# The map from the conditions in steps of two row blocks by 1536 columns, with the next step's loads issued behind each step

## The chip, the cores and the metric

The kernel runs on one core of a Trainium2 chip. The metric is the device time of one execution in microseconds (us). Engine names are those of the profile: PE is TensorE (matmuls; PEld is its weight load), DVE is VectorE, ACT is ScalarE, POOL is GpSimd, SP is the engine whose queue issues the DMAs.

## The reference, cut to what matters

A two-layer trunk over 512 latent and 256 context tokens (768 in all, width 1024). Each layer is FFN, mixer, FFN, and every sub-layer is modulated by shift, scale and gate vectors that are a linear map of two condition vectors (`c` and `c_ctx`):

```
def ada_mod(cond, w, b):                      # w: 1024 x 9216 for each layer
    m = jax.nn.silu(cond) @ w + b
    return m.reshape(m.shape[:-1] + (N_MOD, D_MODEL))

def ffn_half(h, m, j, g, w1, w3, w2):
    u = modulate(rmsnorm(h, g), m[:, :, 3 * j], m[:, :, 3 * j + 1])
    return h + 0.5 * m[:, :, 3 * j + 2] * swiglu(u, w1, w3, w2)
```

The change concerns `ada_mod`: two rows times a matrix of 1024 x 9216 float32, twice. The matrices are 36 MB each in memory and all of them has to be read; the arithmetic is small.

## The kernel before

All activations lie feature-major, with 384 tokens as one chunk. A matmul of the FFNs is done as three matmuls on split operands (`mm3`, lines L197, L198 and L199: high x high, high x low, low x high), 128x128 weights against 384 columns. Weights come from HBM as tiles of 128 x 1024 (`load`, L151, tile name raw) and are split in two by ACT (L191) and DVE (L192) into blocks (blk); POOL forms sums of weight quarters first (`seven`, L574, tile name S). An FFN (`ffn`, L628) goes over 11 groups of two hidden tiles: for each group `up` with w1 (seven products of 12 matmuls), `down` of the group before (96 matmuls), and `up` with w3. The gated values of a group lie in tiles g, from a pool of six.

The map from the conditions is spread over the two FFNs of layer 0 as filling work: FFN(0, 0) carries the rest of layer 0's map (columns 2048 to 9216), FFN(0, 1) all of layer 1's. `ada_round(l, col, ncol)` (L242) is a generator. It goes over the eight row blocks k of 128 rows; for each it loads the row block's columns in tiles of 128 x 1024 (L253, tile name ada, two of them for 2048 columns) and does four matmuls (L257) with the 32-wide stationary operand `sc[:, k, :]`. The four take a quarter of the columns each and write PSUM partitions 0, 32, 64 and 96 of one bank, so that they use four different column groups of the array. A float32 matmul of this kind has two records in the profile: a step of four shows as x8. After the eighth row block `ada_out` copies the bank to SBUF (DVE, L270, tile adasb), transposes it by quarters of 128 columns on PE (L272) and adds the bias (L275).

What sets the order: `ffn` calls `step()` behind every product of `up` and behind every second row of `down`; each `every`-th call advances the generator by one `yield`, that is, by one row block. `every` is 4; in FFN(0, 0) it is 2 in the first group and 1 in the `up` of the second. FFN(0, 0) runs one round of 1024 columns (the gate, which its own first `down` needs) and three of 2048, FFN(0, 1) four of 2048 and one of 1024: 32 and 40 row blocks. The loads of a row block stand in the program at the row block's own matmuls. The two ada tiles come from the pool `more` (two tiles of 128 x 1024), so a load has to wait until the matmuls that read its tile before are through. SP issues all loads in one queue, the weights' and the map's, and a DMA that waits for its tile holds those behind it. The order within each engine is then laid down at build time by a list scheduler, which may move an instruction ahead of or behind others by its own model of when its operands are there.

Of the kernel before, what the change touches and what calls it, by code (L numbers as in the profile page):

```python
# [9 lines left out]
F32 = mybir.dt.float32  # L10
F32R = mybir.dt.float32r
# [5 lines left out]
P = 128  # L17
D = 1024
KD = 8
# [6 lines left out]
NMOD = 9  # L26
# [63 lines left out]
class Builder:  # L90
# [58 lines left out]
    def load(self, src, pool=None):  # L149
        raw = (pool or self.rawp).tile([P, 1024], F32, tag="raw", name=self.name("raw"))  # L150
        self.nc.sync.dma_start(out=raw[:, :src.shape[-1]], in_=src)  # L151
        return raw
# [86 lines left out]
        nc.sync.dma_start(out=self.xs[1], in_=t["xT"][:, :, SEQ:TOK])  # L239


    def ada_round(self, l, col, ncol):  # L242

        nc, t = self.nc, self.t
        w = ncol // 4
        nq = w // P
        ps = self.aux_ps()
        for k in range(KD):

            raws = []  # L250
            for c0 in range(0, ncol, 1024):
                raws.append(self.ada_tile())
                nc.sync.dma_start(  # L253
                    out=raws[-1], in_=t["ada_w"][l, k * P:(k + 1) * P, col + c0:col + c0 + 1024])
            for g in range(4):
                c = g * w
                nc.tensor.matmul(  # L257
                    ps[32 * g:32 * g + 32, :w], self.sc[:, k, :], raws[c // 1024][:, c % 1024:c % 1024 + w],
                    start=(k == 0), stop=(k == KD - 1),
                )  # L260
            yield
        b0 = col // P
        view = lambda x: x[..., b0:b0 + 4 * nq].rearrange("p (s g q) -> p s g q", s=2, g=2)
        self.ada_out(l, ps, w, self.aux_ps(), view)

    def ada_out(self, l, ps, w, pt, view):

# [360 lines left out]
    def ffn(self, l, s, T, after, ready=None, chs=CH2, fill=(), start=None):  # L628
        nc, t = self.nc, self.t
        fill = list(fill)  # L630
        gate = lambda cond, d: self.gh[l][s][:, cond, d:d + 1]
        w = chs[0][1]
# [9 lines left out]
        def step(every=4):  # L642
            turns[0] += 1
            if turns[0] % every == 0:
                next(todo, None)

        with ExitStack() as st:
            self.psum(mm=6)
            pool = lambda name, bufs: st.enter_context(
                self.tc.tile_pool(name=self.name(name), bufs=bufs, reuse_waits="tile"))  # L650
# [2 lines left out]
            self.blocks_in("AAAABBBBB", pool("blkB", 5))  # L653

            whole = chs is CHX2
            gp = pool("g", 4 if whole else 6)
            self.sums = pool("sums", 2)

            more = pool("more", 2)
            nraw = 5  # L660
            if fill:
                self.adap, nraw = more, 3
# [66 lines left out]
            for n in range(NG):  # L729
                last = n == NG - 1  # L730
                g = [[None, None] for _ in range(2)]
# [12 lines left out]
                def room():  # L744
                    if whole:
                        for i in range(2):
                            both = gp.tile([P, 2, 2 * w], F32R, tag="g", name=self.name("g"))
                            g[i] = [both[:, :, :w], both[:, :, w:], both]
                        return
                    for c in range(2):  # L750
                        for i in range(2):
                            g[i][c] = gp.tile([P, 2, w], F32R, tag="g", name=self.name("g"))


                often = lambda: step((2, 1)[n] if n < 2 and start is not None else 4)
                def results(c, fs, ps):
                    for (i, z), p in zip(fs, ps):
                        (first if z == "w1" else second)(i, c, p[:, :w])
                        often()
# [7 lines left out]
                if n == 0:  # L767

                    room()
                    fs = [(i, z) for i in range(2) for z in ("w1", "w3")]  # L770
                    if start is None:
# [5 lines left out]
                    else:  # L777
# [5 lines left out]
                        ps = [self.mm_ps() for _ in fs]  # L783
# [14 lines left out]
                else:  # L798
                    self.up(blocks, T, w, first, often)
                    items = [take(2) for _ in pending], of(pending)  # L800
                    self.down(*items, chs[:1] if last else CHX if whole else chs, gate, step=step)
                    room()
                    self.up(blocks, T, w, second, often)
                if last:
# [667 lines left out]
    def run(self):  # L1472
        t = self.t
        self.setup()
        self.load_x()
        T, begin = self.halves(0, 0, two=True)

        def start():

            begin(*CH2[0])  # L1480
            slot = lambda: self.slot([P, 1024], F32, "ada")
            self.ada_tile = lambda: self.adap.tile([P, 1024], F32, tag="raw", name=self.name("ada"))
            for _ in self.ada_half(0, [slot] * 8):
                pass
            self.now()
            yield
            raw = lambda: self.rawp.tile([P, 1024], F32, tag="raw", name=self.name("ada"))
            half = self.ada_half(1, [slot] * 4 + [raw] * 3 + [self.ada_tile])
            next(half)
            yield  # L1490
            next(half, None)
            yield
            self.load_rest()
            begin(*CH2[1])
            yield

        def rounds(l, first):
            for col in range(first, NMOD * D, 2048):
                yield lambda col=col: self.ada_round(l, col, min(2048, NMOD * D - col))

        def gate():
            yield from self.ada_round(0, 2048, 1024)
            self.ada_gh(0, 0)

        def derive(l):
            def f():
                self.ada_gh(l, 1)
                for j in range(1 - l, 3):
                    self.ada_sp(l, j)
                if l:  # L1510
                    self.ada_gh(1, 0)
            return f

        ffn = lambda l, s: self.ready([t["w1"][l, s, 0], t["w3"][l, s, 0]])
        nxt, after = self.norm(0, 1)
        ready = self.ready([t["ein"][12 + i] for i in range(2)])
        self.ffn(0, 0, T, after, ready, fill=[gate, *rounds(0, 3072), derive(0)], start=start)
        u, (nxt, after) = nxt, self.halves(0, 2)
        self.even_mixer(u[0], after, ffn(0, 1))
        u, (nxt, after) = nxt, self.halves(1, 0)  # L1520
        self.ffn(0, 1, u, after, ffn(1, 0), fill=[*rounds(1, 0), derive(1)])
        u, (nxt, after) = nxt, self.norm(1, 1)
        self.ffn(1, 0, u, after, self.ready([t["oin"][1 + i, 0] for i in range(2)]))
        u, (nxt, after) = nxt, self.halves(1, 2)
        self.odd_mixer(u[0], after, ffn(1, 1))
        self.ffn(1, 1, nxt, self.final(), chs=CHX2)
        self.now()
# [96 lines left out]
```

## Time and profile before

| | |
|---|---|
| time, three runs | 2882.99 us median (2879.05 to 2884.05) |
| the profiled execution | 2885.63 us, span 2883.8 us |
| PE busy | 2798.5 us (97%), 17014 instructions |
| DVE, ACT, POOL busy | 72%, 42%, 17% |
| granted PE clock | 0.99 |
| DMA | 266.38 MB, 92 GB/s over the span |

The map's matmuls stand between 49.2 and 1379.4 us. Three stretches are used below: 100 to 212 us (the first two rounds of 2048 columns, in FFN(0, 0)), 212 to 290 us (the third), and 990 to 1390 us (layer 1's map, in FFN(0, 1)).

### The profile page before, as it was taken

To read this page: it belongs to the slowest core of one execution; us is meant where nothing else is said; L and a number is where in the kernel's file an instruction comes from. 1 tells how busy PE (TensorE), PEld (TensorE's weight loads), DVE (VectorE), ACT (ScalarE), POOL (GpSimd) and SP (SyncE) were. 2 spreads that over 40 slices of the span, in tenths; PEclk is the share of its full clock that TensorE was granted. 3 is DMA by queue.
4 is the path that set the end of the run, shared out by engine and by line. 5 is a ranking of instruction groups with operands and counts; after the bars stand their busy time and mean duration, and the time that the engine had idled before them with its cause. 6 is when DMAs were issued, how large, how long until landed. Compare 5 with 4: busy or idle time off the path is not lost.

```text
span 2883.8 us, 43969 instructions
## 1 busy us (share of the span) xinstructions
PE 2798.5 (97%) x17014; PEld 2603.0 (90%) x17014; DVE 2079.2 (72%) x3994; ACT 1220.1 (42%) x2406; POOL 481.5 (17%) x358
## 2 busy tenths in 40 slices
PE   6999999999999999999999999999999999889998
PEld 5678999999977888889999999999989989789998
DVE  5646777776677776666778777777855565799998
ACT  4323333352166632332336333323564565554443
POOL 0211222200000022121211222222000000133331
PEclk9999999999999999999999999999999999999999
DMA  7564121221110244443221221221121111122332
GB/s 258 162 197 167 59 81 59 70 72 59 54 34 16 74 175 154 175 168 125 96 81 37 81 74 59 81 66 59 61 75 59 59 67 52 66 81 95 110 103 74
DMA packets 81458, 266.38 MB, mean 92 GB/s; under 512 B 8416, under 2 KB 13920, under 8 KB 81248
## 3 DMA queue, kind: packets, MB, share of 16 engines
q1 hardware_dynamic: 81248, 263.56, 26.6%
q8 instruction: 134, 2.20, 0.3%
q14 instruction: 76, 0.62, 0.1%
HBM read 261.43 MB, written 2.10 MB: 91 GB/s over the span
## 4 chain that ended last, share of the span: by engine, by line
PE 87%; DVE 7%; ACT 3%; issue 1%; POOL 1%; DMA 1%; POOLq 0%; SPq 0%; DVEq 0%; ACTq 0%
PE mm L197 27%; PE mm L199 26%; PE mm L198 26%; PE aux L257 3%; DVE blk L192 1%; DVE xx L447 1%; PE o L1040 1%; POOL S L574 1%; DMA ada<-in_ada_w 1%; DVE acc L371 1%; PE aux L1028 1%; PE aux L350 0%; PE ds L1273 0%; PE o L1295 0%; PE aux L1268 0%
## 5 line engine op out<-in xcount | busy, mean ns | idle before, releaser
L192 DVE TENSOR_TENSOR blk<-raw,blk 128x512 fp32r<-128x512 f32 (+1 forms) x617 | 469.2, 769 | 182.9 <-ACT blk L191 175.6
L191 ACT ACTIVATE blk<-raw 128x512 fp32r<-128x512 f32 (+1 forms) x617 | 379.7, 625 | 485.2 <-PE mm L199 417.4
L191 ACT ACTIVATE blk<-S 128x512 fp32r<-128x512 f32 x320 | 201.6, 630 | 560.4 <-PE mm L199 528.6
L197 PE MATMUL mm<-g,blk 128*128 128x384 f32 (+2 forms) x1264 | 429.0, 341 | 3.9 <-ACT blk L191 3.9
L199 PE MATMUL mm<-g,blk 128*128 128x384 f32 (+2 forms) x1264 | 428.2, 339 | 0.0
L198 PE MATMUL mm<-g,blk 128*128 128x384 f32 (+2 forms) x1264 | 427.9, 339 | 0.0
L447 DVE SCALAR_TENSOR_TENSOR xx<-mm,gh,xx 128x384 f32<-128x384 f32 (+3 forms) x600 | 307.3, 519 | 150.4 <-PE mm L199 141.7
L192 DVE TENSOR_TENSOR blk<-S,blk 128x512 fp32r<-128x512 f32 x320 | 252.4, 790 | 90.0 <-ACT blk L191 84.1
L603 DVE TENSOR_TENSOR t<-t,mm 128x384 f32<-128x384 f32 (+1 forms) x400 | 206.8, 517 | 113.2 <-PE mm L199 112.2
L197 PEld LDWEIGHTS mm<-g,blk 128*128 128x128 f32 x1264 | 237.2, 188 | 27.3 <-issue 7.1
L199 PEld LDWEIGHTS mm<-g,blk 128*128 128x128 f32 x1264 | 237.5, 188 | 9.4 <-issue 3.4
L198 PEld LDWEIGHTS mm<-g,blk 128*128 128x128 f32 x1264 | 237.8, 188 | 8.2 <-issue 2.5
L197 PE MATMUL mm<-uH,blk 128*128 128x384 f32 (+1 forms) x648 | 225.9, 353 | 1.8 <-ACT uH L387 1.7
L198 PE MATMUL mm<-uL,blk 128*128 128x384 f32 (+1 forms) x648 | 222.6, 345 | 0.0
L199 PE MATMUL mm<-uH,blk 128*128 128x384 f32 (+1 forms) x648 | 221.9, 345 | 0.0
L574 POOL TENSOR_TENSOR S<-raw 128x512 f32<-128x512 f32 x80 | 114.1, 1426 | 583.5 <-DMA raw<-in_w 399.9
L574 POOL TENSOR_TENSOR S<-raw,raw 128x512 f32<-128x512 f32 x80 | 106.2, 1328 | 458.2 <-DVE blk L192 457.2
L574 POOL TENSOR_TENSOR S<-S,raw 128x512 f32<-128x512 f32 x80 | 109.9, 1374 | 319.5 <-issue 314.4
L191 ACT ACTIVATE g<-t 128x384 fp32r<-128x384 f32 (+1 forms) x176 | 87.1, 497 | 129.8 <-DVE t L741 128.6
L197 PEld LDWEIGHTS mm<-uH,blk 128*128 128x128 f32 x648 | 121.1, 188 | 10.3 <-ACT uH L387 3.1
L199 PE MATMUL mm<-T11H,blk 128*128 128x384 f32 (+1 forms) x384 | 126.1, 329 | 3.9 <-DVE blk L192 3.9
L197 PE MATMUL mm<-T21H,blk 128*128 128x384 f32 (+1 forms) x384 | 125.8, 330 | 3.8 <-ACT t L608 1.9
(282 smaller groups left out, 6937.9 us busy)
## 6 DMA issues: line engine op xcount, KB each, us to landing
raw<-in_w SPq DMA_DIRECT2D x256, 512.0 KB, 3.3
ada<-in_ada_w SPq DMA_DIRECT2D x144, 512.0 KB, 4.4
raw<-in_oin SPq DMA_DIRECT2D x32, 512.0 KB, 3.2
raw<-in_w SPq DMA_DIRECT2D x32, 256.0 KB, 2.8
raw<-in_ein SPq DMA_DIRECT2D x16, 512.0 KB, 3.3
raw<-in_eout SPq DMA_DIRECT2D x8, 512.0 KB, 3.2
raw<-in_oi SPq DMA_DIRECT2D x8, 512.0 KB, 3.2
raw<-in_oout SPq DMA_DIRECT2D x8, 512.0 KB, 3.2
```

Source lines behind the costliest of these rows:

```text
L191: self.nc.scalar.activation(out=hi, in_=src, func=AF.Copy)
L192: (eng or self.nc.vector).tensor_tensor(out=lo, in0=src, in1=hi.bitcast(F32), op=ALU.subtract)
L197: nc.tensor.matmul(out, aH, bH, start=start, stop=False, skip_group_check=more)
L198: nc.tensor.matmul(out, aH, bL, start=False, stop=False, skip_group_check=more)
L199: nc.tensor.matmul(out, aL, bH, start=False, stop=stop, skip_group_check=more)
L257: nc.tensor.matmul(ps[32 * g:32 * g + 32, :w], self.sc[:, k, :], raws[c // 1024][:, c % 1024:c % 1024 + w], start=(k == 0), stop=(k == KD ...
L371: nc.vector.tensor_tensor(out=acc[:, :w], in0=acc[:, :w], in1=dst[:, :w], op=ALU.add)
L447: nc.vector.scalar_tensor_tensor(out=xv, in0=ps[:, off:off + m], scalar=gate(cond, d), in1=xv, op0=ALU.mult, op1=ALU.add,)
L574: nc.gpsimd.tensor_tensor(out=out, in0=a, in1=b, op=op)
L603: add = lambda out, a, b: nc.vector.tensor_tensor(out=out, in0=a, in1=b, op=ALU.add)
L1028: nc.tensor.transpose(pt[:, k * P:(k + 1) * P], pr[:, (k0 + k) * P:(k0 + k + 1) * P], self.ident)
L1040: nc.tensor.matmul(o[64 * e:64 * e + 64, :256], V[kt // 3][:, kt % 3, c:c + 64], s.PT[e][:, k, :], start=k == 0, stop=k == nk - 1)
```

## The change

`ada_round` becomes `ada_rounds(l, jobs)`. A job is a range of columns and a function to call when its values are there; FFN(0, 0) has one job of 1024 and four of 1536 columns, FFN(0, 1) six of 1536. A step is two row blocks (eight matmuls) of one tile each, so an FFN has 20 and 24 steps. The loads of the next step, also the next job's, stand behind the matmuls of a step. `ada_out` follows at once behind a job's last step instead of at the next `yield`. The ada tiles are 128 x 1536 (two, in `more`); the pool g has four tiles in these two FFNs instead of six, and the last group's gated values of the second chunk lie in the two tiles of `more`. `step()` advances the map every second call in the first group and every sixth call of `up` afterwards; the calls in `down` stay at every fourth. Outside these two FFNs the order of every engine is the same as before.

```diff
-    def ada_round(self, l, col, ncol):
+    def ada_rounds(self, l, jobs):
...
-        for k in range(KD):
+        def load(col, ncol, k):
             raws = []
-            for c0 in range(0, ncol, 1024):
+            for kk in (k, k + 1):
                 raws.append(self.ada_tile())
                 nc.sync.dma_start(
-                    out=raws[-1], in_=t["ada_w"][l, k * P:(k + 1) * P, col + c0:col + c0 + 1024])
-            for g in range(4):
-                c = g * w
-                nc.tensor.matmul(
-                    ps[32 * g:32 * g + 32, :w], self.sc[:, k, :], raws[c // 1024][:, c % 1024:c % 1024 + w],
-                    start=(k == 0), stop=(k == KD - 1),
-                )
+                    out=raws[-1][:, :ncol], in_=t["ada_w"][l, kk * P:(kk + 1) * P, col:col + ncol])
+            return raws
+
+        steps = [(*job, k) for job in jobs for k in range(0, KD, 2)]
+        raws = load(*steps[0][:2], 0)
+        for i, (col, ncol, done, k0) in enumerate(steps):
+            w = ncol // 4
+            if k0 == 0:
+                ps = self.aux_ps()
+            for k, raw in zip((k0, k0 + 1), raws):
+
+                for g in range(4):
+                    nc.tensor.matmul(
+                        ps[32 * g:32 * g + 32, :w], self.sc[:, k, :], raw[:, g * w:(g + 1) * w],
+                        start=(k == 0), stop=(k == KD - 1),
+                    )
+            if i + 1 < len(steps):
+                raws = load(*steps[i + 1][:2], steps[i + 1][3])
+            if k0 == KD - 2:
+                b0, nq = col // P, w // P
+                view = lambda x: x[..., b0:b0 + 4 * nq].rearrange("p (s g q) -> p s g q", s=2, g=2)
+                self.ada_out(l, ps, w, self.aux_ps(), view)
+                if done:
+                    done()
             yield
...
-            gp = pool("g", 4 if whole else 6)
+            gp = pool("g", 4 if whole or fill else 6)
...
+            lent = lambda: (more if fill else gp).tile(
+                [P, 2, w], F32R, tag="raw" if fill else "g", name=self.name("g"))
...
-                            g[i][c] = gp.tile([P, 2, w], F32R, tag="g", name=self.name("g"))
+                            g[i][c] = lent() if last and c else gp.tile(
+                                [P, 2, w], F32R, tag="g", name=self.name("g"))
...
-                often = lambda: step((2, 1)[n] if n < 2 and start is not None else 4)
+                often = lambda: step(2 if n == 0 else 6)
...
-            self.ada_tile = lambda: self.adap.tile([P, 1024], F32, tag="raw", name=self.name("ada"))
+            self.ada_tile = lambda: self.adap.tile([P, 1536], F32, tag="raw", name=self.name("ada"))
...
-        self.ffn(0, 0, T, after, ready, fill=[gate, *rounds(0, 3072), derive(0)], start=start)
+        self.ffn(0, 0, T, after, ready, fill=[rounds(0, [(2048, 1024, lambda: self.ada_gh(0, 0))])], start=start)
...
-        self.ffn(0, 1, u, after, ffn(1, 0), fill=[*rounds(1, 0), derive(1)])
+        self.ffn(0, 1, u, after, ffn(1, 0), fill=[rounds(1, [])])
```

Three places in the order of the instructions. Names carry the buffers' numbers; aux is the map's PSUM bank, mm a bank of the FFN.

PE, FFN(0, 0), in the first `down` (the matmuls on g), where the first 2048-column round runs before and the first 1536-column job now. Before:

```order
L198 MATMUL mm_180_1035<-g_7_130,blk_160_932 128x384
L257 MATMUL aux_155_917<-ada_165_973,sc_85 32x512 x2
L199 MATMUL mm_180_1035<-g_7_130,blk_160_932 128x384
L197 MATMUL mm_180_1035<-g_8_131,blk_168_985 128x384
L198 MATMUL mm_180_1035<-g_8_131,blk_168_985 128x384
L199 MATMUL mm_180_1035<-g_8_131,blk_168_985 128x384
L257 MATMUL aux_155_917<-ada_166_975,sc_85 32x512 x2
L197 MATMUL mm_181_1043<-g_7_130,blk_164_958 128x384
```

In the changed kernel, at the same place:

```order
L198 MATMUL mm_184_1080<-g_10_133,blk_166_977 128x384
L199 MATMUL mm_184_1080<-g_10_133,blk_166_977 128x384
L264 MATMUL aux_155_904<-ada_175_1019,sc_85 32x384 x4
L264 MATMUL aux_155_904<-ada_176_1021,sc_85 32x384 x4
L197 MATMUL mm_187_1101<-g_9_132,blk_162_940 128x384
L198 MATMUL mm_187_1101<-g_9_132,blk_162_940 128x384
```

The four matmuls of one row block, which stood in two pairs with four of the FFN's between them, now stand together, and the next row block's four stand right behind them.

PE, FFN(0, 0), at the end of the first group, where the gate's 1024 columns end. Before, the last three row blocks:

```order
L257 MATMUL aux_89_483<-ada_141_816,sc_85 32x256 x3
L197 MATMUL mm_129_780<-T1H_100_541,blk_138_796 128x384
L198 MATMUL mm_129_780<-T1L_101_542,blk_138_796 128x384
L257 MATMUL aux_89_483<-ada_144_840,sc_85 32x256 x4
L197 MATMUL mm_130_781<-T2H_114_623,blk_140_801 128x384
L198 MATMUL mm_130_781<-T2L_115_624,blk_140_801 128x384
L257 MATMUL aux_89_483<-ada_146_861,sc_85 32x256 x4
L257 MATMUL aux_89_483<-ada_150_886,sc_85 32x256 x4
```

In the changed kernel, from the gate's last step on:

```order
L264 MATMUL aux_91_487<-ada_123_716,sc_85 32x256 x4
L264 MATMUL aux_91_487<-ada_124_718,sc_85 32x256 x4
L197 MATMUL mm_136_815<-T11H_41_235,blk_145_829 128x384
L198 MATMUL mm_136_815<-T11L_42_236,blk_145_829 128x384
L197 MATMUL mm_137_816<-T1H_104_557,blk_146_832 128x384
L198 MATMUL mm_137_816<-T1L_105_558,blk_146_832 128x384
L197 MATMUL mm_138_817<-T2H_118_639,blk_148_837 128x384
L198 MATMUL mm_138_817<-T2L_119_640,blk_148_837 128x384
L284 MATMUL aux_130_787<-ident_81,adasb_131_788 128x128 x2
L264 MATMUL aux_155_904<-ada_128_783,sc_85 32x384 x4
```

The gate's transposes (L284, the former L272) and the first row block of the next job now stand six of the FFN's matmuls behind the gate's last step; before, the transposes stood 55 rows behind it.

SP, the same time: the loads of the gate's last row blocks and of the round or job behind it. Before:

```order
L253 DMA ada_146_861<-in_ada_w 128x1024
L253 DMA ada_150_886<-in_ada_w 128x1024
L253 DMA ada_156_918<-in_ada_w 128x1024
L253 DMA ada_157_920<-in_ada_w 128x1024
L151 DMA raw_158_928<-in_w2 128x1024
L151 DMA raw_159_930<-in_w3 128x1024
L151 DMA raw_167_983<-in_w3 128x1024
L151 DMA raw_170_991<-in_w1 128x1024
L253 DMA ada_161_947<-in_ada_w 128x1024
L253 DMA ada_162_949<-in_ada_w 128x1024
```

In the changed kernel:

```order
L251 DMA ada_124_718<-in_ada_w 128x1024
L251 DMA ada_128_783<-in_ada_w 128x1536
L251 DMA ada_129_785<-in_ada_w 128x1536
L251 DMA ada_156_913<-in_ada_w 128x1536
L151 DMA raw_160_936<-in_w2 128x1024
L151 DMA raw_161_938<-in_w3 128x1024
L151 DMA raw_165_975<-in_w3 128x1024
L251 DMA ada_157_915<-in_ada_w 128x1536
L151 DMA raw_168_983<-in_w1 128x1024
```

A weight tile of the next `down` (raw_160, before raw_158) now stand behind the first load of a job's second step, which waits for the matmuls on ada_128.

## Rows read from the trace of the kernel before

**Rows 1.** The page's first part (busy us, share of the span, instructions) and the lines of its chain of work that ended last.

```profile
PE 2798.5 (97%) x17014; PEld 2603.0 (90%) x17014; DVE 2079.2 (72%) x3994; ACT 1220.1 (42%) x2406; POOL 481.5 (17%) x358
...
PE mm L197 27%; PE mm L199 26%; PE mm L198 26%; PE aux L257 3%; DVE blk L192 1%; DVE xx L447 1%; PE o L1040 1%; POOL S L574 1%; DMA ada<-in_ada_w 1%; DVE acc L371 1%; PE aux L1028 1%; PE aux L350 0%; PE ds L1273 0%; PE o L1295 0%; PE aux L1268 0%
```

**Rows 2.** Busy time by stretch, all engines (columns: stretch, its us, then busy us and instructions of PE, PEld, DVE, ACT, POOL, then granted PE clock, DMA share, GB/s).

```profile
100.00:212.00 112.00, 108.44 (x547) 75.81 (x547) 54.55 (x106) 24.09 (x43) 21.53 (x16) 0.98 0.59 194
...
990.00:1390.00 400.00, 398.36 (x2341) 356.27 (x2342) 270.33 (x519) 134.60 (x254) 79.55 (x60) 1.00 0.44 154
```

**Rows 3.** The same stretches for the map's matmuls alone (L257; busy us of PE and PEld, then clock, DMA share, GB/s).

```profile
100.00:212.00 112.00, 31.41 (x128) 4.26 (x128) 0.98 0.59 194
212.00:290.00 78.00, 8.52 (x64) 1.26 (x64) 1.00 0.47 162
990.00:1390.00 400.00, 40.24 (x320) 6.42 (x320) 1.00 0.44 154
```

**Rows 4.** PE in order of time (start, us, instruction; xN counts records): a step of 512 columns whose four matmuls stand together, between the FFN's.

```profile
222.65 0.33 PE L197 MATMUL mm<-T4H,blk 128*128 128x384 f32 x1
...
223.00 0.34 PE L199 MATMUL mm<-T4H,blk 128*128 128x384 f32 x1
223.27 1.06 PE L257 MATMUL aux<-ada,sc 128*32 128x512 f32 x8
...
224.54 0.34 PE L198 MATMUL mm<-T11L,blk 128*128 128x384 f32 x1
```

**Rows 5.** The same view, a step in two halves.

```profile
115.18 0.34 PE L198 MATMUL mm<-g,blk 128*128 128x384 f32 x1
115.45 1.05 PE L257 MATMUL aux<-ada,sc 128*32 128x512 f32 x4
116.43 0.45 PE L199 MATMUL mm<-g,blk 128*128 128x384 f32 x1
116.71 0.34 PE L197 MATMUL mm<-g,blk 128*128 128x384 f32 x1
...
117.34 1.05 PE L257 MATMUL aux<-ada,sc 128*32 128x512 f32 x4
```

**Rows 6.** The same view: a step of 256 columns; and, ahead of it in the program, 31 matmuls of 256 columns in a row (L295, the part of the map that is done before FFN(0, 0)).

```profile
1324.12 0.34 PE L199 MATMUL mm<-T2H,blk 128*128 128x384 f32 x1
1324.38 0.64 PE L257 MATMUL aux<-ada,sc 128*32 128x256 f32 x8
...
1325.24 0.34 PE L198 MATMUL mm<-T21L,blk 128*128 128x384 f32 x1
...
36.58 3.65 PE L295 MATMUL mm<-ada,sc 128*32 128x256 f32 x62
```

**Rows 7.** The same view: three of PE's four waits for a load of the map, and what follows (in brackets the idle time ahead and what ended it).

```profile
85.35 0.64 PE L257 MATMUL aux<-ada,sc 128*32 128x256 f32 x8 [1.69 <-DMA ada<-in_ada_w]
87.28 1.08 PE L257 MATMUL aux<-ada,sc 128*32 128x256 f32 x8 [1.29 <-DMA ada<-in_ada_w]
88.29 0.69 PE L199 MATMUL mm<-T11H,blk 128*128 128x384 f32 x1
...
90.69 0.34 PE L197 MATMUL mm<-T11H,blk 128*128 128x384 f32 x1
...
107.35 1.59 PE L257 MATMUL aux<-ada,sc 128*32 128x512 f32 x4 [2.58 <-DMA ada<-in_ada_w]
108.87 0.69 PE L199 MATMUL mm<-T4H,blk 128*128 128x384 f32 x1
...
110.45 1.37 PE L257 MATMUL aux<-ada,sc 128*32 128x512 f32 x4
```

**Rows 8.** PE's waits from 45 to 300 us (us in total, times, longest).

```profile
PE aux L257 <- DMA ada<-in_ada_w: 6.5, 4, 2.6
```

**Rows 9.** The copy of a finished bank on DVE, its neighbours there, and the transposes behind it on PE; then a set of transposes that stands alone.

```profile
1236.34 1.14 DVE L192 TENSOR_TENSOR blk<-raw,blk 128x512 fp32r<-128x512 f32 x1
...
1237.86 0.68 DVE L270 COPY adasb<-aux 128x512 f32<-128x512 f32 x1
...
1238.60 0.66 PE L272 MATMUL aux<-ident,adasb 128*128 128x128 f32 x4 [0.18 <-DVE adasb L270]
...
289.82 0.34 PE L199 MATMUL mm<-T22H,blk 128*128 128x384 f32 x1
290.00 0.60 PE L272 MATMUL aux<-ident,adasb 128*128 128x128 f32 x4
...
290.61 0.34 PE L198 MATMUL mm<-T4L,blk 128*128 128x384 f32 x1
```

**Rows 10.** SP in order of time (its DMA issues), the loads' median time to landing from 990 to 1390 us, and a POOL instruction that waits for the weights issued at 1086.48.

```profile
1085.58 0.80 SPq L253 DMA_DIRECT2D ada<-in_ada_w  x2
1086.48 0.37 SPq L151 DMA_DIRECT2D raw<-in_w  x1
...
ada<-in_ada_w SPq DMA_DIRECT2D x70, 512.0 KB, 4.2
raw<-in_w SPq DMA_DIRECT2D x48, 512.0 KB, 3.5
...
1091.93 1.29 POOL L574 TENSOR_TENSOR S<-raw 128x512 f32<-128x512 f32 x1 [6.83 <-DMA raw<-in_w]
```

**Rows 11.** Who waited for whom from 1000 to 1390 us, the largest wait (us in total, times, longest).

```profile
ACT blk L191 <- PE mm L199: 195.7, 71, 13.4
```

More of the change, by code (lines that the diff above doesn't have):

```diff
@@ L239, in load_rest @@
         nc.sync.dma_start(out=self.xs[1], in_=t["xT"][:, :, SEQ:TOK])
-    def ada_round(self, l, col, ncol):
+    def ada_rounds(self, l, jobs):
         nc, t = self.nc, self.t
-        w = ncol // 4
-        nq = w // P
-        ps = self.aux_ps()
-        for k in range(KD):
+        def load(col, ncol, k):
             raws = []
-            for c0 in range(0, ncol, 1024):
+            for kk in (k, k + 1):
                 raws.append(self.ada_tile())
                 nc.sync.dma_start(
-                    out=raws[-1], in_=t["ada_w"][l, k * P:(k + 1) * P, col + c0:col + c0 + 1024])
-            for g in range(4):
-                c = g * w
-                nc.tensor.matmul(
-                    ps[32 * g:32 * g + 32, :w], self.sc[:, k, :], raws[c // 1024][:, c % 1024:c % 1024 + w],
-                    start=(k == 0), stop=(k == KD - 1),
-                )
+                    out=raws[-1][:, :ncol], in_=t["ada_w"][l, kk * P:(kk + 1) * P, col:col + ncol])
[20 more added lines that the diff above has]
+                    done()
             yield
-        b0 = col // P
-        view = lambda x: x[..., b0:b0 + 4 * nq].rearrange("p (s g q) -> p s g q", s=2, g=2)
-        self.ada_out(l, ps, w, self.aux_ps(), view)
     def ada_out(self, l, ps, w, pt, view):
@@ L1487, in start @@
             raw = lambda: self.rawp.tile([P, 1024], F32, tag="raw", name=self.name("ada"))
-            half = self.ada_half(1, [slot] * 4 + [raw] * 3 + [self.ada_tile])
+            half = self.ada_half(1, [slot] * 4 + [raw] * 3 + [lambda: self.ada_tile()[:, :1024]])
             next(half)
@@ L1495, in start, with rounds, derive @@
             yield
[L1497 to L1506, printed above, removed]
+        def rounds(l, jobs):
+            def derive():
                 self.ada_gh(l, 1)
@@ L1511, in f @@
                     self.ada_gh(1, 0)
-            return f
+            first = jobs[-1][0] + jobs[-1][1] if jobs else 0
+            jobs = jobs + [(col, 1536, None) for col in range(first, NMOD * D, 1536)]
+            jobs[-1] = *jobs[-1][:2], derive
+            return lambda: self.ada_rounds(l, jobs)
         ffn = lambda l, s: self.ready([t["w1"][l, s, 0], t["w3"][l, s, 0]])
```

## The prediction

> **What bounds the kernel now.** I read the engines' totals first: PE is busy 97% of the span, and the chain that ended last is made of its matmuls, 3% of it the map's [rows 1]. So time is won only where PE does less or waits less. The stretches come next. In 990 to 1390 us, where layer 1's map runs, PE is busy 398.4 of 400 us while DVE has 270 and ACT 135; from 100 to 212 us it is busy 108.4 of 112 [rows 2]. PE is the limit in both, and what the change takes from PE there is time, as long as the weights still come. The reader should then look at how the map's matmuls lie between the FFN's: what counts is how often PE is interrupted, more than how many columns it is given.
>
> **What an interruption costs.** Take the start of the FFN matmul ahead of a run of the map's and the start of the second one behind it, less two ordinary spacings. An ordinary spacing is 0.175 us (222.65 to 223.00 us for two). A run of four matmuls of 512 columns costs 224.54 - 223.00 - 0.35 = 1.19 us [rows 4]. A run of only two of the four costs 116.71 - 115.18 - 0.35 = 1.18 us, and its other half comes at 117.34 and costs as much again [rows 5]: the four column groups work side by side, so half a step costs a whole one. Four matmuls of 256 columns cost 1325.24 - 1324.12 - 0.35 = 0.77 us. From 256 to 512 columns the price rises by 0.42 us, so the fixed part of a run is 0.35 us. Where 31 matmuls of 256 columns stand in a row (62 records) they take 3.65 us, that is 0.47 us for four [rows 6]: nearly the 0.42 of the columns, with the fixed part paid once. Four of 384 columns alone therefore cost 0.35 + 0.63 = 0.98 us, and eight in a row 0.35 + 1.26 = 1.61 us (estimates from these rows).
>
> A rule that speaks against the change: the Trainium skill, TensorEngine Tiling (Array Packing), section Performance Considerations, says that each matmul carries some 60 cycles of its own. The change makes 352 matmuls of the map out of 288 for the same columns; by the page's figure 64 more would be an estimated 1.6 us at 2.4 GHz, and the sum below would be smaller by that. The 31 in a row show no such part per matmul, so I don't take it.
>
> **PE's work, part by part.** The columns are the same before and after; the runs are not.
> - FFN(0, 0), the 2048-column rounds: 24 row blocks in 37 runs (14 in the first round, first at 100.01 us; 15 in the second; 8 in the third). The busy time says so too: 31.4 us for the 16 row blocks of the first two rounds against 8.5 us for the 8 of the third [rows 3]. 37 x 1.19 = 44.0 us. In the changed order 15 of the 16 steps of 1536 columns stand in one run and the other in three: 15 x 1.61 + 3 x 0.98 = 27.1 us. Gain 16.9 us.
> - The gate's 1024 columns: nine runs of 0.77, now five and two double ones (0.77 + 0.42): 6.9 to 6.2, gain 0.7 us.
> - FFN(0, 1): 33 runs of 512 and 8 of 256 columns, 39.3 + 6.2 = 45.5 us (busy 40.2 [rows 3], the rest being the spacing lost around them). Now 22 of 24 steps in one run and two in two each: 22 x 1.61 + 4 x 0.98 = 39.3 us. Gain 6.2 us.
>
> Together 23.8 us. The transposes are the same 32 tiles in 11 sets instead of 9; a set of four alone takes 290.61 - 289.82 - 0.35 = 0.44 us, 0.11 each, with no fixed part [rows 9], so more sets cost nothing.
>
> **The waits that go.** PE waited four times, 6.5 us in all, for a load of the map [rows 8], all in FFN(0, 0). Behind a wait it runs at half speed for a while: from 88.29 to 90.69 us seven matmuls take 2.40 us instead of 1.3, the run at 87.28 takes 1.01 instead of 0.57, the run at 107.35 1.52 instead of 0.98, and the four behind it 1.58 instead of 0.9 [rows 7]. That is the lower of the two clock levels, 1.2 instead of 2.4 GHz, and another 2.8 us. With the loads a step ahead, and 10 to 15 us between steps (50 or 75 FFN matmuls and a run), against a median landing of 4.2 us [rows 10], these 9.3 us go.
>
> **The waits that come.** Two.
> - The first 1536-column step stands six FFN matmuls and two transposes behind the gate's last step, whose tiles its loads need. They can be issued only when the gate's matmuls are through, and PE is there about 2 us later (six spacings, the transposes and the wait for their copy); a load takes 3.5 to 4.2 us from issue to landing [rows 10] and is half as long again here. The wait is 0 to 3.5 us; I take 1.5, nearer to the short landing, and 1.3 for half speed behind it. Queued behind PE is the whole FFN; on SP the weights behind `ada_156` wait too, but those are for the next `down`, seven products later.
> - The transposes now stand five FFN matmuls (0.9 us) behind a job's last step and need DVE's copy. Copying 512 columns takes 0.68 us, and PE waited 0.18 us for one that DVE reached late [rows 9]. For 384 columns DVE needs about 0.55 us and just makes it when it is free; if it has just begun its longest neighbour (1.14 us [rows 9]) PE loses about 1.0 us. Eleven sets: 0 to 11 us; I take 0.2 each, 2.2 us, as in the row that shows such a wait.
>
> The smaller pool g costs nothing: a group's tiles are written behind the `down` that frees them, four products of the next `up` later. The `more` tiles that the last group borrows are free by then, since 24 steps end in about the sixth group. The loads have the same bytes.
>
> **The sum.** 2885.6 - 23.8 - 6.5 - 2.8 + 1.5 + 1.3 + 2.2 = 2857.5 us against the profiled execution, 28.1 us less. The median of the runs lies 2.6 us below that execution: **2855 us**.
>
> **Rivals.**
> - *The new waits eat half.* Every copy comes late (11 us) and the map's loads are waited for as before (9.3 us): 2883 - 23.8 - 9.3 + 11 + 9.3 = 2870 us. For it: DVE is busy 68% where the map runs. Against it: in `down`, where most jobs end, DVE only drains PSUM rows that PE finished before the run.
> - *Two row blocks don't share a run.* Each pays its own 0.35 us: 37 x 0.35 = 13 us less gain, 2868 us. Against it speak the 31 in a row [rows 6].
> - *The change doesn't bring what it should:* PE's freed time comes back as waits for weights that ACT, DVE or POOL deliver no faster than now; 2880 us. Against it: ACT waited 195.7 us for PE to free a block between 1000 and 1390 us [rows 11], so it is ahead.
> - *Slower: weights behind the map's loads.* SP issues in one queue. A weight tile issued behind two loads of 512 KB at 1086.48 let POOL begin at 1091.93, 5.45 us later, against a median landing of 3.5 [rows 10]: 2 us for 1 MB, so 3 us for the 1.5 MB now (estimate). And up to two steps' loads now stand between two weight tiles, so that the second is held for 10 to 15 us more. It costs only where ACT's lead is used up: from there, some 20 weight tiles (two of six in each of the ten groups with map) 2.5 us late would be 50 us: 2883 - 28 + 50 = 2905 us. By the Trainium skill, DMA: Bandwidth & Descriptors, section Queues, rings and completion order, descriptors of one queue are taken in ring order, so that what stands behind waits; the 5.45 us agree. ACT's waits for PE, up to 13.4 us [rows 11], speak against it.
>
> **How the numbers follow.** Forecast 0.67, new waits 0.12, no shared runs 0.08, nothing gained 0.07, slower 0.06. A measurement of this kernel can tell about 0.2%, 5.8 us. Faster by more than that are the first three, 0.87; within it 0.07; slower 0.06. The forecast's own ends are 2850 (no new wait at all) and about 2865; three us below for the spread of the runs, and up through the two rivals at 2868 and 2870 with some room: 2847 to 2876.
>
> **What would show it.** In the changed profile the map's runs should read x16, with some 1.4 us from their start to the next FFN matmul and 1.6 us by the rule of three starts above; in the stretches of rows 3 the map's matmuls should fall from 80 to about 60 busy us. PE's waits for the map's loads should be one or two near the end of the first group. A wait of PE for adasb at the 11 transposes shows the copies' price. ACT waiting for the weights' DMA instead of PE, and PE for blk, would show the slower case. The prediction is wrong if runs of eight cost two runs, or if PE's idle time grows by more than 10 us between 80 and 1400 us.

## The result, and the profile after

The changed kernel takes 2854.01 us (median of 4 runs, 2852.49 to 2856.89) against 2882.3 us of the kernel before on the same chip (2879.05 to 2884.05): 28.3 us less, a ratio of 0.9903 [0.9891, 0.9915]. The profiled execution took 2852.72 us and its span is 2850.9 us, 32.9 us less than the span before. The forecast was 2855 us.

The first lines to read are the engines' totals and the chain that ended last, to be laid beside [rows 1].

```profile
PE 2771.3 (97%) x17142; PEld 2605.0 (91%) x17142; DVE 2082.8 (73%) x4000; ACT 1218.7 (43%) x2406; POOL 479.9 (17%) x358
...
PE mm L197 27%; PE mm L198 26%; PE mm L199 26%; PE aux L264 2%; DVE blk L192 1%; DVE xx L459 1%; PE o L1056 1%; POOL S L586 1%; PE aux L1044 1%; PE aux L362 1%; PE o L1311 1%; PE ds L1289 0%; PE aux L1284 0%; ACT blk L191 0%; PE aux L339 0%
```

PE has 128 more records and 27.2 us less busy time; its idle time in the span went from 85.3 to 79.6 us. So 27 of the 33 us are busy time of PE, not waits: 17.2 up to the end of FFN(0, 0), 6.9 in the stretch with FFN(0, 1), and 3.1 in stretches where the two kernels have the same order. The other engines do what they did. In the chain the map's matmuls went from 3 to 2%, and the map's loads, 1% before, are gone from it.

The next line groups the map's matmuls (us busy and mean ns, then the idle time ahead of them); before, the same view had 86.8 us for x576 at L257.

```profile
L264 PE MATMUL aux<-ada,sc 128*32 128x384 f32 (+1 forms) x704 | 68.3, 487 | 1.7 <-DMA ada<-in_ada_w 1.7
```

The same weights pass PE in 18.5 us less. Of the rest of the 27.2 us, the 3.1 of the unchanged stretches owe nothing to the change; some 5.6 lie in the FFN's matmuls around the runs (the spacing that each interruption stretches) and in those that ran at the lower clock.

Now PE in order of time, four places: a step of the map between the FFN's matmuls, a step that was cut in two, the transposes of a finished bank, and the end of the gate with the first step of the next job.

```profile
143.77 0.34 PE L199 MATMUL mm<-T4H,blk 128*128 128x384 f32 x1
144.03 1.50 PE L264 MATMUL aux<-ada,sc 128*32 128x384 f32 x16
145.46 0.44 PE L197 MATMUL mm<-T11H,blk 128*128 128x384 f32 x1
145.74 0.34 PE L198 MATMUL mm<-T11L,blk 128*128 128x384 f32 x1
...
1196.48 0.34 PE L199 MATMUL mm<-T11H,blk 128*128 128x384 f32 x1
1196.75 0.85 PE L264 MATMUL aux<-ada,sc 128*32 128x384 f32 x8
...
1197.82 0.34 PE L198 MATMUL mm<-T1L,blk 128*128 128x384 f32 x1
...
285.58 0.34 PE L198 MATMUL mm<-g,blk 128*128 128x384 f32 x1
285.75 0.49 PE L284 MATMUL aux<-ident,adasb 128*128 128x128 f32 x3
...
286.26 0.33 PE L197 MATMUL mm<-g,blk 128*128 128x384 f32 x1
...
84.53 0.34 PE L198 MATMUL mm<-T2L,blk 128*128 128x384 f32 x1
85.71 0.44 PE L284 MATMUL aux<-ident,adasb 128*128 128x128 f32 x2 [0.85 <-DVE adasb L282]
87.51 1.25 PE L264 MATMUL aux<-ada,sc 128*32 128x384 f32 x8 [1.36 <-DMA ada<-in_ada_w]
89.35 0.69 PE L199 MATMUL mm<-T11H,blk 128*128 128x384 f32 x1 [0.59 <-DVE blk L192]
...
92.39 0.53 PE L199 MATMUL mm<-T11H,blk 128*128 128x384 f32 x1
92.84 1.49 PE L264 MATMUL aux<-ada,sc 128*32 128x384 f32 x2
...
94.71 0.34 PE L199 MATMUL mm<-T1H,blk 128*128 128x384 f32 x1
```

By the rule of three starts the run of eight costs 145.74 - 143.77 - 0.35 = 1.62 us, the run of four 1197.82 - 1196.48 - 0.35 = 0.99, and three transposes 286.26 - 285.58 - 0.35 = 0.33. The last rows, from 84.53 us on, are the one place where the changed kernel waits long in the map (there is one more wait, of 0.32 us, at 59.76). The clock there is seen in the view by stretches (stretch, its us, busy us and instructions of PE, PEld, DVE, ACT, POOL, granted PE clock, DMA share, GB/s); the row from 100 to 212 us answers to the first of [rows 2].

```profile
82.50:89.30 6.80, 4.05 (x33) 1.80 (x32) 6.80 (x19) 2.90 (x7) 0.00 (x0) 0.89 0.62 231
89.30:94.30 5.00, 4.95 (x13) 3.29 (x13) 3.67 (x7) 0.67 (x2) 2.36 (x2) 0.50 0.44 157
...
100.00:212.00 112.00, 112.00 (x709) 99.57 (x708) 73.55 (x134) 34.06 (x61) 25.38 (x19) 1.00 0.56 200
```

From 82.5 to 89.3 us PE is busy 4.05 of 6.80 us; in the 5 us behind, its granted clock is 0.50, the lower level of 1.2 GHz. From 100 to 212 us it is busy all the time, where it lost 3.6 us before. DVE is busy for the whole of 82.50 to 89.30.

What PE waited for from 45 to 300 us, and what ACT waited for from 965 to 1240 us (us, times, longest):

```profile
PE aux L264 <- DMA ada<-in_ada_w: 1.7, 2, 1.4
...
PE aux L284 <- DVE adasb L282: 0.8, 1, 0.8
...
ACT blk L191 <- PE mm L199: 120.9, 43, 14.5
```

The map's loads cost PE 1.7 us instead of 6.5 [rows 8]. One of the eleven sets of transposes waits for its copy. ACT still waits for PE to free a block, up to 14.5 us at a time: weights are ahead of PE as they were [rows 11]; in the same stretch they landed in a median of 3.4 us, the map's loads of 768 KB in 5.4.

Where along the span the time was won is read from DMA issues that both kernels have: the first load of the even mixer's rope table stands behind FFN(0, 0), the last load of in_eout ahead of FFN(0, 1), the first of in_oin behind FFN(1, 0). The rows of the loads by tensor (issue time, least, median and greatest in ns, then first and last start), first of the kernel before:

```profile
L841 SPq DMA_DIRECT2D rope<-in_rope x1: 526/526/526, 616.5 to 616.5; - x1
...
L151 SPq DMA_DIRECT2D raw<-in_eout x8: 327/328/328, 670.4 to 869.8; - x8
...
L151 SPq DMA_DIRECT2D raw<-in_oin x32: 327/328/328, 2026.7 to 2422.5; - x32
```

and of the changed kernel:

```profile
L857 SPq DMA_DIRECT2D rope<-in_rope x1: 525/525/525, 594.7 to 594.7; - x1
...
L151 SPq DMA_DIRECT2D raw<-in_eout x8: 327/328/328, 648.5 to 846.5; - x8
...
L151 SPq DMA_DIRECT2D raw<-in_oin x32: 327/328/328, 1996.6 to 2392.1; - x32
```

FFN(0, 0) ends 616.5 - 594.7 = 21.8 us earlier. From the last in_eout to the first in_oin it was 1156.9 us and is 1150.1: 6.8 us in FFN(0, 1). Together 28.6 us, close to the 28.3 between the medians. The other 4.3 us of the spans lie in stretches in which the two kernels have the same order; they are missing from the changed kernel's second profile, e0 below.

The same three numbers for every kernel that was run (us; the rest is the span less the two):

| kernel | to the first rope load | last in_eout to first in_oin | rest | median time |
|---|---|---|---|---|
| before | 616.5 | 1156.9 | 1110.4 | 2882.3 |
| changed | 594.7 | 1150.1 | 1106.1 | 2854.0 |
| e0_after | 595.9 | 1150.5 | 1110.0 | 2857.5 |
| e1_single | 601.0 | 1155.0 | 1110.4 | 2868.2 |
| e3_rate | 605.2 | 1157.0 | 1109.6 | 2871.7 |
| e5_1024 | 598.3 | 1154.7 | 1108.6 | 2863.2 |
| e2_own | 592.8 | 1150.3 | 1109.9 | 2855.2 |
| e6_onegroup | 595.2 | 1149.9 | 1110.9 | 2853.9 |
| e7_lateout | 596.1 | 1150.9 | 1108.7 | 2858.0 |
| e9_twoloads | 595.9 | 1153.6 | 1108.3 | 2860.4 |

The rest varies by 1 to 5 us without any cause in the code, so the two stretches tell more than the median. e0, e1, e3 and e5 ran beside the kernel before at 2881.68 us (2875.89 to 2884.29), the other four on another chip beside 2882.48 us (2879.77 to 2885.36).

### The profile page after: what moved, and what is told of

The parts are those of the page before. It is cut to its first block, busy times and chain, and to the rows that moved or that the text cites. A ratio compares the mean times of both kernels' runs of the same rounds, so it can differ in the third digit from the quotient of the medians.

```text
span 2850.9 us, 44146 instructions
## 1 busy us (share of the span) xinstructions
PE 2771.3 (97%) x17142; PEld 2605.0 (91%) x17142; DVE 2082.8 (73%) x4000; ACT 1218.7 (43%) x2406; POOL 479.9 (17%) x358
## 3 DMA queue, kind: packets, MB, share of 16 engines
q1 hardware_dynamic: 75488, 263.56, 26.5%
## 4 chain that ended last, share of the span: by engine, by line
PE 88%; DVE 7%; ACT 3%; issue 1%; POOL 1%; DMA 0%; SPq 0%; POOLq 0%; DVEq 0%; ACTq 0%
PE mm L197 27%; PE mm L198 26%; PE mm L199 26%; PE aux L264 2%; DVE blk L192 1%; DVE xx L459 1%; PE o L1056 1%; POOL S L586 1%; PE aux L1044 1%; PE aux L362 1%; PE o L1311 1%; PE ds L1289 0%; PE aux L1284 0%; ACT blk L191 0%; PE aux L339 0%
## 5 line engine op out<-in xcount | busy, mean ns | idle before, releaser
L192 DVE TENSOR_TENSOR blk<-raw,blk 128x512 fp32r<-128x512 f32 (+1 forms) x617 | 475.3, 779 | 172.5 <-ACT blk L191 162.5
```

What stands on the lines that cost most here:

```text
L192: (eng or self.nc.vector).tensor_tensor(out=lo, in0=src, in1=hi.bitcast(F32), op=ALU.subtract)
```

## The experiments

The theory: an interruption has a fixed price of 0.35 us, and the change wins by having fewer of them (23.8 us) and by not waiting for the map's loads (9.3 us with the slow clock behind). Rivals: the loads a step ahead are what brings it; the number or the columns of the matmuls, not the runs, set the price; the larger transfers bring it; and for what is lost, the copies.

**e0_after.** The changed kernel once more, on the chip and in the rounds of the first three experiments.

> The changed kernel once more, beside the others on one chip: 28 us less than the kernel before by the sum of runs and waits; every theory expects the 0.990 that was measured.

2857.46 us (2854.99 to 2863.54), ratio 0.9921 [0.9908, 0.9934]. That is 24.2 us less by the medians (19.0 to 26.5 by its interval), where 28 were expected. The two intervals overlap, and by the marks the two FFNs win 20.6 + 6.4 = 27.0 us.

**e1_single.** The changed kernel with steps of one row block, at twice the rate: the same matmuls, columns and loads, in more runs.

```diff
-            for kk in (k, k + 1):
+            for kk in (k,):
...
-        steps = [(*job, k) for job in jobs for k in range(0, KD, 2)]
+        steps = [(*job, k) for job in jobs for k in range(KD)]
...
-            for k, raw in zip((k0, k0 + 1), raws):
+            for k, raw in zip((k0,), raws):
...
-            if k0 == KD - 2:
+            if k0 == KD - 1:
...
-                    step()
+                    step(2)
...
-                often = lambda: step(2 if n == 0 else 6)
+                often = lambda: step(1 if n == 0 else 3)
```

> The changed kernel with steps of one row block instead of two, at twice the rate, each step's one load behind the step before. Bytes, columns and the loads' lead stay; 77 runs of the map's matmuls stand where 44 stood for the 1536-column jobs (71 of four, 4 of eight, 2 parts, against 37 of eight and 7 smaller). If the price is that of a run (0.35 us fixed): 71 x 0.98 + 4 x 1.61 + 2 x 0.98 = 77.9 instead of 66.4 us, so 11.5 us slower than the changed kernel, 16 to 17 us faster than the one before. If the gain came from loads issued ahead: no difference to the changed kernel.

2868.19 us (2866.53 to 2873.98), ratio 0.996 [0.9948, 0.9973], 10.7 us above e0. By the marks it loses 6.3 us in FFN(0, 0) and 4.9 in FFN(0, 1) against the changed kernel's first profile, 5.1 and 4.5 against e0. A step on PE:

```profile
213.06 0.34 PE L199 MATMUL mm<-T3H,blk 128*128 128x384 f32 x1
213.33 0.85 PE L264 MATMUL aux<-ada,sc 128*32 128x384 f32 x8
...
214.39 0.34 PE L198 MATMUL mm<-T22L,blk 128*128 128x384 f32 x1
```

1.33 - 0.35 = 0.98 us. Two of them cost 1.96, the run of eight 1.62: sharing a run saves 0.34 us, and the experiment takes that back, in the trace and in the time. The number of interruptions is a cause, and its size is the one forecast.

**e3_rate.** The kernel before with one number altered: in the second group the map goes on at every call, in the product with w3 at every fourth, where it stood at every call too. Fewer half steps, no other change.

```diff
-                often = lambda: step((2, 1)[n] if n < 2 and start is not None else 4)
+                often = lambda: step((2, 1)[n] if start is not None and (n == 0 or n == 1 and not gate_done) else 4)
```

(`gate_done` is set behind each group's product with w1.)

> The kernel before with one thing changed: in the second group of FFN(0, 0), behind the first up, the map advances with every fourth call instead of every one. Runs of 512-column matmuls fall from 70 to 61, since fewer steps are torn in two. By the price of a run: 9 x 1.19 = 10.7 us faster than before. If the waits for the loads are the greater part: 6 to 9 us faster, with the four waits gone; if the tearing costs nothing: no difference or only the waits'.

2871.72 us (2869.71 to 2873.53), ratio 0.9968 [0.9955, 0.998], 10.0 us below the kernel before. By the marks 11.3 us come from FFN(0, 0) and none from FFN(0, 1), which it leaves alone. PE's waits for the map's loads in 45 to 300 us:

```profile
PE aux L257 <- DMA ada<-in_ada_w: 3.9, 3, 1.9
```

3.9 us, so 2.6 of the 10 to 11 us were a wait; the busy time of the map's matmuls fell from 86.8 to 77.0 us. With the wait, nine runs fewer should have given 10.7 + 2.6 = 13.3 us. The gate's two waits stayed and grew (1.93 and 1.67 us, before 1.69 and 1.29), and the granted clock behind them was 0.50 from 88.7 to 98 us, before 0.51 from 87.2 to 90.7; that takes some of it back, so this run bears out the direction and no more than the rough size. Half of FFN(0, 0)'s gain was to be had without larger steps: there the kernel before had interrupted itself twice for each row block [rows 5].

**e5_1024.** The changed kernel with jobs of 1024 columns: runs of eight matmuls of 256 columns, more of them.

```diff
-            jobs = jobs + [(col, 1536, None) for col in range(first, NMOD * D, 1536)]
+            jobs = jobs + [(col, 1024, None) for col in range(first, NMOD * D, 1024)]
-                often = lambda: step(2 if n == 0 else 6)
+                often = lambda: step(2 if n == 0 else 4)
...
-                    step()
+                    step(3)
```

> The changed kernel with jobs of 1024 columns instead of 1536, two row blocks a step as before, loads ahead as before: 60 runs of eight 256-column matmuls instead of 37 of eight 384-column ones. By the price of a run: 60 x 1.19 + 9 x 0.77 = 78.3 instead of 72.6 us, 5.7 us slower than the changed kernel. If larger loads are what brings the gain: slower by more than 10 us. If the loads' lead is: no difference.

2863.2 us (2860.48 to 2864.28), ratio 0.9937 [0.9924, 0.9951], 5.7 us above e0, 6.6 by the marks. A run:

```profile
206.25 0.34 PE L199 MATMUL mm<-T21H,blk 128*128 128x384 f32 x1
206.52 1.07 PE L264 MATMUL aux<-ada,sc 128*32 128x256 f32 x16
...
207.80 0.34 PE L198 MATMUL mm<-T3L,blk 128*128 128x384 f32 x1
```

1.55 - 0.35 = 1.20 us, where the price list (0.35 and twice 0.42) says 1.19. The list holds for columns, for row blocks and for the number of runs.

**e2_own.** The loads of a step issued at the step itself, not behind the step ahead of it.

```diff
-        raws = load(*steps[0][:2], 0)
         for i, (col, ncol, done, k0) in enumerate(steps):
             w = ncol // 4
+            raws = load(col, ncol, k0)
...
-            if i + 1 < len(steps):
-                raws = load(*steps[i + 1][:2], steps[i + 1][3])
```

> The changed kernel with the loads of a step issued at the step itself, in the program's order, instead of behind the step before; runs as in the changed kernel (37 of eight). If the gain is the runs': within 2 us of the changed kernel, since SP comes to a load early and a load can start only when the matmuls on its tile are through, in either place. If the gain is the loads issued ahead: 9 us slower than the changed kernel or more, with waits of PE for them.

2855.16 us (2854.15 to 2856.19), ratio 0.9904 [0.989, 0.9917]: no loss. PE's waits for the map's loads, from 45 to 300 and from 930 to 1400 us:

```profile
PE aux L264 <- DMA ada<-in_ada_w: 1.5, 1, 1.5
...
PE aux L264 <- DMA ada<-in_ada_w: 1.8, 2, 1.3
```

e0, with the loads ahead in the program, has 1.4 and 2.2. But the edit did not take the lead away. SP's loads of two row blocks in the kernel before, in the changed kernel, and in e2 with the step ahead of them:

```profile
224.36 0.81 SPq L253 DMA_DIRECT2D ada<-in_ada_w  x2
...
144.95 0.97 SPq L251 DMA_DIRECT2D ada<-in_ada_w  x2
...
142.13 1.50 PE L264 MATMUL aux<-ada,sc 128*32 128x384 f32 x16
...
143.05 0.97 SPq L251 DMA_DIRECT2D ada<-in_ada_w  x2
```

In all three the loads are issued about 1 us behind the start of a step's matmuls (223.27 [rows 4], 144.03, 142.13) and serve the step after it: SP is there early, and the tiles decide. The new place in the program is worth nothing, since the loads went out a step ahead in the kernel before too; what a kernel without that lead would lose wasn't run. That leaves the larger distance between steps as the reason why waits went, which is argued from rows and not shown by a run of its own. Before, PE reached the second step of the first round 4.8 us behind the start of the one at 100.01 and waited 2.58 us for a load issued at 101.10 [rows 7]; the changed kernel's steps there start at 100.22, 109.54 and 119.50. With e1's smaller distance one wait of 1.06 us is back, at 116.11.

**e6_onegroup.** Here part of the map is left out: in seven of the eight row blocks of each job, three of the four matmuls (three of the four column groups), so that the map's values aren't the reference's. Runs, loads and copies stay.

```diff
-                for g in range(4):
+                for g in range(4 if k == 0 else 1):
...
-                        start=(k == 0), stop=(k == KD - 1),
+                        start=(k == 0), stop=(k == KD - 1 or g > 0),
```

> The changed kernel with three of the four matmuls left out in seven of the eight row blocks of each job (the map's values are then wrong). If the four column groups work side by side, the time stays within 3 us of the changed kernel. If each matmul costs its own columns, three quarters of seven eighths of the columns' part (about 57 us) go: 37 us faster.

2853.94 us (2848.86 to 2857.84), ratio 0.9898 [0.9885, 0.9912]: the time of the changed kernel, with a third of its records (x242 for x704). A run:

```profile
158.69 0.34 PE L199 MATMUL mm<-T22H,blk 128*128 128x384 f32 x1
158.96 1.48 PE L264 MATMUL aux<-ada,sc 128*32 128x384 f32 x4
...
160.65 0.34 PE L198 MATMUL mm<-T4L,blk 128*128 128x384 f32 x1
```

1.96 - 0.35 = 1.61 us for two matmuls, one per row block, against 1.62 for eight. The three groups left out cost nothing, since they run beside the first. The Trainium skill, TensorEngine Tiling (Array Packing), section Key Properties, says that tiles of the array operate independently, and that changing the tiling mode drains the engine. The 1.61 beside 1.62 us agree with the first; the fixed 0.35 us would fit the second, but no run here tells a drain from another fixed cost.

**e7_lateout.** The copy and the transposes of a finished job moved to the start of the next step, so that DVE has that long for the copy (all jobs but the gate and the last).

```diff
+        out = None
...
+            if out:
+                out()
+                out = None
...
-                self.ada_out(l, ps, w, self.aux_ps(), view)
+                def out(ps=ps, w=w, view=view, done=done):
+                    self.ada_out(l, ps, w, self.aux_ps(), view)
+                    if done:
+                        done()
                 if done:
-                    done()
+                    out()
+                    out = None
```

> The changed kernel with the copy and the transposes of a finished job put behind the next step's start, as in the kernel before (the gate's and the last job's stay). If PE's waits for the copy cost what the prediction put down (0.2 us each): 2 us faster; by the trace of the changed kernel, which shows one such wait of 0.85 us at the gate: no difference, within 1 us.

2858.03 us (2856.76 to 2860.23), ratio 0.9915 [0.9902, 0.9929]; 596.1 and 1150.9 us by the marks, beside 595.9 and 1150.5 of e0. Nothing is won; by the median it is 2.9 us above e2 of the same rounds. But for the gate's copy, which this run leaves in its place, no copy was waited for, so there was nothing to take away; in FFN(0, 1) one set even waits longer, 1.7 us.

**e9_twoloads.** Each load of 1536 columns issued as three of 512, into the same tile. Bytes, tiles and order stay.

```diff
-                nc.sync.dma_start(
-                    out=raws[-1][:, :ncol], in_=t["ada_w"][l, kk * P:(kk + 1) * P, col:col + ncol])
+                for c in range(0, ncol, 512):
+                    nc.sync.dma_start(out=raws[-1][:, c:c + 512], in_=t["ada_w"][l, kk * P:(kk + 1) * P, col + c:col + c + 512])
```

> The changed kernel with each load of 1536 columns issued as three of 512 columns: the same bytes, three times the DMAs, rows of 2 KB instead of 6 KB. If the gain is the runs': within 2 us of the changed kernel. If larger loads bring it: 10 us slower or more, with waits of PE for the map's loads or for the weights.

2860.39 us (2858.92 to 2861.85), ratio 0.9922 [0.9908, 0.9935]. That is 5.2 us above e2 of the same rounds, more than the 2 expected and far from the 10 of the rival. By the marks FFN(0, 0) is where e0 has it, and FFN(0, 1) 3.1 to 3.5 us longer. PE's waits for the map's loads don't show that (1.0 and 1.6 us, fewer than e0's). They lie inside the runs, where the weight load of a matmul (PEld) waits for its part of a row block. From 930 to 1400 us, e2 and e9:

```profile
PEld aux L264 <- DMA ada<-in_ada_w: 3.2, 2, 2.0
...
PEld aux L265 <- DMA ada<-in_ada_w: 6.9, 10, 2.3
```

That is 3.7 us more, in ten waits instead of two; the run of eight at 1028.02 reads 3.78 us instead of 1.50. The larger loads are worth about 3 us against three small ones each, not the gain.

Steps of four row blocks would halve the number of runs once more. They need four tiles of 128 x 1536 instead of two, and weren't tried.

## Why the prediction was right

The sum, 28.1 us against 28.3, is nearer than the runs allow: e0, the same kernel, won 24.2 us by the medians and 27.0 by the marks. Its largest term is shown; among the smaller ones errors cancel.

**The runs, 23.8 us: right, in price and in number.** The price that the forecast put together from runs of four, 1.61 us for eight of 384 columns, was measured at 1.62; 0.98 for a single one at 0.98 and 0.99. e1 gives 0.34 us back for every run that it cuts in two and loses 10.7 us, e5 follows the same list in another shape. What made this possible is that the list was taken from starts of the FFN's matmuls on both sides of a run, not from busy time: mean busy ns of a map matmul (564 before, 487 after) would not have told a fixed part from a part per column.

**By stage.** The forecast's terms give 17.6 + 9.3 - 2.8 - 1.0 (five copies) = 23.1 us in FFN(0, 0) and 6.2 - 1.2 (six) = 5.0 in FFN(0, 1). Measured were 21.8 and 6.8. FFN(0, 1) won what its runs are worth (6.4 us in e0), since its copies cost nothing. FFN(0, 0) won 20.6 us in e0 and 23.7 in e2, so its 21.8 can't be split finer than 1 or 2 us.

**The waits that go, 9.3 us: gone as forecast, with half of the reason wrong.** PE's waits for the map's loads fell from 6.5 to 1.7 us, and the slow clock behind the wait at 107.35 us is gone. "With the loads a step ahead, and 10 to 15 us between steps": the first half of that sentence explains nothing, since the loads were issued a step ahead before the change as well (e2); the second half fits the rows and has no run of its own.

**The first step of the new job, 2.8 us: too small.** The wait is 1.36 us, as forecast (1.5). But PE then waits 0.59 us for DVE's block, and the granted clock is 0.50 for the 5.0 us behind, where it was 0.51 for 3.5 us (87.2 to 90.7) before. Ten FFN matmuls from 89.35 to 92.39 us at 0.34 us each cost 3.04 - 9 x 0.175 = 1.5 us more, and the run at 92.84 1.97 instead of 0.98, another 1.0. Together 4.4 us. From start to start it is a little more: the 10.18 us from 84.53 to 94.71 hold 12 spacings, two transposes and two runs of 0.98, 4.3 us by the prices above. Of the 5.9 us lost, 0.85 are the copy's and 5.0 this term's; the first run, at 87.51, was slow already (1.25 us for 0.85). How long the clock stays low differs from one execution to the next. The same place in e0:

```profile
86.83 0.34 PE L198 MATMUL mm<-T2L,blk 128*128 128x384 f32 x1
...
89.89 1.42 PE L264 MATMUL aux<-ada,sc 128*32 128x384 f32 x8 [1.43 <-DMA ada<-in_ada_w]
91.65 0.69 PE L199 MATMUL mm<-T11H,blk 128*128 128x384 f32 x1 [0.34 <-DVE blk L192]
...
95.45 0.34 PE L199 MATMUL mm<-T1H,blk 128*128 128x384 f32 x1
```

By the same count that is 8.62 - 4.3 - 0.85 = 3.5 us (also in e2), not 5.0. What was missed is DVE and how long the clock stays low. DVE in order of time:

```profile
85.24 0.42 DVE L282 COPY adasb<-aux 128x256 f32<-128x256 f32 x1
...
86.51 0.23 DVE L287 TENSOR_TENSOR mT<-aux,pk 128x8 f32<-128x8 f32 x2
...
87.12 0.17 DVE L326 TENSOR_SCALAR gh<-mT 128x16 f32<-128x16 f32 x1
87.20 1.49 DVE L192 TENSOR_TENSOR T3L<-Tf,T3H 128x384 fp32r<-128x384 f32 x3
88.61 0.68 DVE L192 TENSOR_TENSOR blk<-raw,blk 128x512 fp32r<-128x512 f32 x1
```

DVE has no idle time from 82.50 to 89.30 us, and the gate's copy and its derived values (L287, L326) now stand ahead of the block that PE waits for at 89.35. That block would be as late with the map's load on time; how much of the 1.36 us would then become a wait for it wasn't tried.

**The copies, 2.2 us: too large.** One of eleven waits, 0.85 us, at the same place. For the rest five FFN matmuls, 0.9 us, were enough. The two terms for new waits, 5.0 us forecast, came to 5.0 + 0.85 = 5.9 in this profile and 3.5 + 0.85 = 4.3 in e0: two errors that largely cancel, which is luck.

**The signs and the rivals.** The runs read x16, with 1.43 us from their start to the next FFN matmul; in the three stretches of [rows 3] the map's matmuls are busy 55.3 us, a little under the 60 expected. New waits that eat half: the copies cost 0.85 of their 11 us, the loads 1.7 of 9.3. No shared runs: 1.62 us, not 1.96. Nothing gained, or weights late: ACT waited 120.9 us for PE in 965 to 1240 us, and 111.0 in the same stretch before, when the map still had 140 us to go; the weights landed in 3.4 us there against 4.0. So the reason that was given against them, ACT's lead, held.

The rule of the Trainium skill, TensorEngine Tiling (Array Packing), section Performance Considerations, on a part of each matmul's own, weighed in the prediction at 1.6 us for 64 more matmuls, left no mark: the run of eight is 0.01 us above the price without it, over 37 runs some 0.4 us (an estimate).

## What to carry to other kernels

Work that is woven into another stream of matmuls is paid for by the interruption as well as by its columns: take its price from the starts of the neighbours on both sides, for two sizes, and split it into a fixed and a growing part. Then count runs, in the order of the instructions, not matmuls; a step that the order cuts in two pays twice, and one number of the rate (e3) was worth a third of the whole change. When a wait is to go, ask which engine is next: right behind the last wait for a load PE stood waiting for DVE. And look in the trace whether an edit moved a transfer at all: in e2 it did not, because the tile's release sets the time of issue.

## What the runs showed of the hardware

- Four matmuls on 32 columns of the array each cost what one of them costs: a run of eight 1.62 us, with one of each four alone 1.61 us (e6), a half set of 512 columns 1.18 and a whole one 1.19 us [rows 4, 5].
- Going from the FFN's 128-wide matmuls to a run of the map's 32-wide ones and back costs 0.35 us whatever the run holds (two row blocks or one; 256, 384 or 512 columns); 128-wide transposes between them carry no such part, 0.33 us for three and 0.44 for four.
- At waits of 0.85, 1.36 and 0.59 us, close together, PE's granted clock was 1.00 up to 87.5 us and 0.50 from 88.8 to 94.3, and a run of one matmul took 1.97 us there. In e0, the same order, the waits were 0.85, 1.43 and 0.34 us; the clock, 0.54 from 91.6 to 93.6 us, was 1.00 from 93.6 to 95.2, and the same run took 0.97.
- The map's loads took their time of issue from their tiles: with two tiles for a step of two loads, moving the load in the program (e2) left the issue at 0.9 us behind the start of the step ahead.
